# A hybrid SSD and attention layer on one core: grouped sample attention, a token-tile first norm, and a new link from w_out to the FFN

## The chip, the cores and the metric

The kernel runs on one core of a Trainium2 chip. The core has a matrix engine (PE, with its weight loads as PEld), a vector engine (DVE), a scalar engine (ACT), GpSimd (POOL), and DMA queues that are issued from SP, ACT or POOL. Each engine takes its instructions in the order of its own list and waits on semaphores for the others. The metric is the device time of one execution in microseconds (us).

## The reference

One step of a decoder layer on 256 prompt tokens and 8 sample tokens (one new token for each of 8 sequences), all in fp32:

```
hn     = rms_norm(x, norm_mix_pre)                    # (264, 2048)
q,k,v,z,xbc,dt,gates = split(hn @ w_in)
attn   = window attention with sinks, 32 heads of 64, 8 K/V heads, window 128
         (sample tokens: 127 cached keys and values of their own sequence, and the new one)
y      = SSD scan of the convolved xbc (prompt), one recurrent step (sample); gated group norm
merged = sigmoid(g_attn)*(attn @ w_attn_branch) + sigmoid(g_ssm)*(y @ w_ssm_branch)
h      = x + rms_norm(merged @ w_out, norm_mix_post)
f      = swiglu(rms_norm(h, norm_ffn_pre) @ w_gate_up) @ w_down
out    = h + rms_norm(f, norm_ffn_post)
```

The outputs are out for both kinds of tokens, and the new attention windows, convolution states and SSD states.

## The kernel before

Activations lie transposed: a matrix of 2048 channels by 264 tokens is 16 chunks of 128 channels by T = 264 tokens (tokens 0 to 255 prompt, 256 to 263 sample). Every product with a weight matrix goes through `gemm` (L142). A number a is split into hi, rounded for the matrix engine's fp32r format, and lo = a - hi, and a product takes three matmuls of a 128x128 weight block with 264 columns: hi·XH, hi·XL and lo·XH (L186 to L188). Per four blocks of rows one 1 MB DMA fills a `raw` buffer (SP's queue, three buffers); in two halves ACT makes `hi` (L176) and DVE makes `lo` (L177), then 24 matmuls a half follow. The whole kernel has 15984 of these matmuls. A matmul in plain fp32 runs in two passes and stands as two instructions in the trace (a transpose as one).

The order of the work is set by a scheduler that follows the program's text and estimated costs; `tc.manual_schedule` and `tc.issue_after` override it. Beside the gemms run generators on a list `side`; `gemm` calls `tick` (L129) after every four blocks, and that lets each generator take some steps.

Three places matter here.

**The start (L215 to L297).** Three tiles `xt` (sample, prompt 0 to 127, 128 to 255) are loaded on SP ahead of the first three raw blocks. ACT and DVE sum their squares (L263, L265). PE transposes each of the 16 chunks (three transposes a chunk, L272), ACT copies each to `xr` (L274), and SP stores it for later. `rsqrt` (L97) is three Newton steps on DVE; `rowcast` (L251) spreads the result over partitions by three fp32 matmuls of two passes each (L253), and DVE copies it to `rbx` (L280). Then DVE makes xf = xr·w·rbx (L283), ACT XH (L92), and POOL XL (L93). The first gemm makes the SSD's B, the second its C.

**Sample attention (L718 to L772), a generator beside the gemm of w_ssm_branch** (matmuls on YH, YL). For each of the 8 sequences: load K (ring `kr` of 3 on POOL's queue) and V, transpose K in four chunks (L732), four score matmuls with K as the stationary operand and 8 columns moving (L738), copy to `sT`. For every four sequences: transpose, softmax on 128 rows, one transpose back (L756), 16 matmuls of 8 columns with V as the stationary operand (L763), and 32 small copies into the attention output `AF` (L769).

**The link from w_out to the FFN (L845 to L919).** While w_out's chunks leave PSUM, ACT squares them and DVE adds the first 12 squares; after the last chunk 15 tiny matmuls (`tokstat`, L865) sum the squares over channels, `rsqrt` makes r1 on 3 columns, and `rowcast` spreads it. Then for each of 16 chunks, on DVE by hand-written order: mw·rb1 (L898), h = xr + mw (L900), HL (L908), with HH and a square on ACT (L901, L902) and a sum `hs` of squares on POOL (L904, L906). The first two column groups of w_gate_up, `gate(0)` and `gate(1)`, follow; their chunk order needs HH and HL one after the other, and their output is multiplied by rb2, the second norm, which two matmuls with a matrix of ones and an `rsqrt` on 264 columns make.

Of the kernel before, what the change touches and what calls it, by code (L numbers as in the profile page):

```python
# [32 lines left out]
def build(tc, I, O, wbufs=(3, 4, 4), gbufs=5, sbufs=((3,), (1,), (3,)), woff=0, aux="gpsimd", rr=1.4, pr=1.2, su=2, sr=1.0, hb=5, xbb=2, x0g=(0, 1, 2, 3), x0st="sync"):  # L33
# [91 lines left out]
    side = []  # L125
    last = [None]
# [19 lines left out]
    def gemm(W, segs, nk, X, perm_heads=False, perm_rows=False):  # L146
# [4 lines left out]
        for g0 in range(0, nk, 4):  # L151
            raw = til(wp, [P, 4, 512], "raw", wbufs[0])
            with tc.high_priority(offset=woff):
# [11 lines left out]
                for b in range(2):  # L165
# [13 lines left out]
            for b in range(2):  # L179
                hi, lo = hl[b]  # L180
                for m in range(nch):
                    for k in range(2):
# [3 lines left out]
                        PE.matmul(ps[m][:, :T], wh, XH[kc], start=f, stop=False)  # L186
# [28 lines left out]
    xts = {}  # L215
    N1 = til(A0, [P, P], "N1")
    for t in (2, 0, 1):
        n = NS if t == 2 else P
        xts[t] = til(A0, [P, D], f"xt{t}")
        dma(xts[t][:n], I["x_prompt"][t * P:t * P + P] if t < 2 else I["x_sample"])  # L220
        if t == 2:
            dma(ident, I["consts"][:, 0:P])
            dma(N1[0:16], I["norm_mix_pre"].rearrange("(c p) -> c p", p=P))
# [7 lines left out]
    ld(cst, I["consts"][:, P:])  # L231
# [15 lines left out]
    ps = sps()  # L247
    PE.transpose(ps[:, 0:16], N1[:16], ident[:16, :16])
    V.tensor_copy(w_pre, ps[:, 0:16])

    def rowcast(cols, ps):  # L251
        for t, n in enumerate((P, P, NS)):
            PE.matmul(ps[:, t * P:t * P + n], cols[:n, t:t + 1].broadcast_to([n, P]), ident[:n, :n], start=True, stop=True)  # L253
        return ps


    ss = til(cp, [P, 3], "ss")
    V.memset(ss, 1.0)
    for t in (2, 0, 1):
        n = NS if t == 2 else P  # L260
        sq = til(A0, [P, D], "sq", 2)
        if t == 1:
            V.tensor_tensor_reduce(sq, xts[t], xts[t], 1.0, 0.0, ALU.mult, ALU.add, ss[:, t:t + 1])  # L263
        else:
            S.activation(sq[:n], xts[t][:n], AF.Square, accum_out=ss[:n, t:t + 1])  # L265
    X0G = x0g
    X0ST = getattr(nc, x0st).dma_start
    xrs = []
    for c in range(16):
        ps = sps()  # L270
# [24 lines left out]
    PE.transpose(ps[:, 0:48], VR[:48], ident[:48, :48])  # L295
# [233 lines left out]
    AF_ = [til(AFp, [P, T], f"AF{c}") for c in range(16)]  # L529
# [188 lines left out]
    def sample_attention():  # L718
        for b4 in range(2):
            Vb = []  # L720
            sT = til(SA, [P, P], "sT", 1)
            for bb in range(4):
                b = 4 * b4 + bb
                kr = til(SA, [P, 512], "kr", 3)
                ld(kr, I["cache_win_k"][b])
                vb = til(SA, [P, 512], "vb", 4)
                ld(vb, I["cache_win_v"][b])
                ld(vb[0:1, :], vn_d[b:b + 1])
                Vb.append(vb)
# [27 lines left out]
            pt = til(SA, [P, P], "spt", 1)
            V.tensor_copy(pt, ps[:, 0:P])
# [42 lines left out]
    for g in range(8):  # L801
# [6 lines left out]
        for i in range(4):  # L808
            c = 4 * g + i
            V.scalar_tensor_tensor(y4[:, i, :], y4[:, i, :], w_ssmn[:, c:c + 1], rb, ALU.mult, ALU.mult)  # L810
            split(y4[:, i, :], YH[c], YL[c])
    side.append([sample_attention(), sr, 0.0])
    for u4 in range(4):
# [42 lines left out]
    mw = [til(EP, [P, T], f"mw{m}") for m in range(16)]  # L856
    xr = [til(EP, [P, T], f"xr{m}") for m in range(16)]
    for m in range(16):
        ld(xr[m], xT_d[m])
    halves = [lambda a: a[:, 0:2], lambda a: a[:NS, 2:3]]  # L860

    def tokstat(ps, accs, first, last):
        for t, n in enumerate((P, P, NS)):
# [251 lines left out]
```

## Time and profile before

| | |
|---|---|
| median of 3 runs | 2171.52 us (2171.44 to 2175.14) |
| the profiled execution | 2174.78 us |
| its span in the profile | 2173.0 us |
| PE busy | 2134.5 us, 98% of the span |
| DVE, ACT, POOL busy | 1380.0, 1105.6, 275.5 us |
| DMA | 442.52 MB, mean 204 GB/s |

Times in the profile count from the start of the span. In a timeline a row is a run of like instructions of one engine: start, time from the first's start to the last's end, engine, line, what it writes and reads, count, and in brackets the idle time before and who ended it. A matmul's duration is longer than its share of the engine, since matmuls overlap; its price is read from one start to the next. The column PEclk is the granted clock of the matrix engine, as a part of its full 2.4 GHz (0.50 is the lower level, 1.2 GHz).

### The profile page before, as it was taken

How to read it: one execution, taken by the hardware profiler on the slowest of the kernel's cores; microseconds unless marked ns; L12 is line 12 of the kernel's file. 1: busy time of each engine (PE TensorE's matmuls, PEld its weight loads, DVE VectorE, ACT ScalarE, POOL GpSimd, SP SyncE). 2: the span in 40 equal slices, each digit the busy share in tenths (PEclk: the TensorE clock that was granted, in tenths of full speed). 3: DMA queues.
4: the chain of work that ended last, by engine and by line, in shares of the span. 5: the costliest groups of instructions: out<-in, count | busy, mean ns of one | idle time of the engine just before them, and what ended most of it. 6: DMA issues, size and time to landing. Idle time of an engine off the chain costs nothing.

```text
span 2173.0 us, 43304 instructions
## 1 busy us (share of the span) xinstructions
PE 2134.5 (98%) x17533; PEld 2103.9 (97%) x17533; DVE 1380.0 (64%) x2764; ACT 1105.6 (51%) x1984; POOL 275.5 (13%) x512
## 2 busy tenths in 40 slices
PE   8999999999999999999999999899999999999997
PEld 6999999999999999999999999899999999999997
DVE  5877776777689988866544554844554545544444
ACT  5555555555478977755433444544444444434442
POOL 4100111111133222223001120300000000000000
PEclk9999999999999999999999999999999999999998
DMA  5655665555587787877567985365655555565552
GB/s 194 230 184 191 197 195 181 190 189 190 176 308 244 251 284 260 287 228 234 173 198 190 219 261 183 118 212 189 208 189 187 194 195 185 180 225 178 175 175 99
DMA packets 216633, 442.52 MB, mean 204 GB/s; under 512 B 12352, under 2 KB 28240, under 8 KB 215656
## 3 DMA queue, kind: packets, MB, share of 16 engines
q1 hardware_dynamic: 194864, 372.51, 53.2%
q0 software_dynamic: 21424, 67.17, 9.4%
q8 instruction: 137, 2.24, 0.4%
q14 instruction: 64, 0.52, 0.1%
q10 hardware_dynamic: 144, 0.07, 0.0%
HBM read 402.81 MB, written 41.45 MB: 204 GB/s over the span
## 4 chain that ended last, share of the span: by engine, by line
PE 91%; DMA 4%; DVE 3%; issue 1%; ACT 1%; POOL 0%; SPq 0%; DVEq 0%; ACTq 0%; POOLq 0%
PE g L186 28%; PE g L188 28%; PE g L187 28%; DMA raw<-in_w_attn_branch 2%; DMA y<-y_d 1%; PE s L272 1%; DVE lo L177 1%; PE w L701 1%; PE w L662 0%; PE w L694 0%; DMA ta_d<-tg 0%; DMA xt<-in_x_prompt 0%; ACT hi L176 0%; PE s L467 0%; DMA ts_d<-tg 0%
## 5 line engine op out<-in xcount | busy, mean ns | idle before, releaser
L177 DVE TENSOR_TENSOR lo<-raw,hi 128x1024 fp32r<-128x1024 f32 (+1 forms) x640 | 776.9, 1217 | 594.4 <-ACT hi L176 588.0
L176 ACT CAST hi<-raw 128x1024 fp32r<-128x1024 f32 (+1 forms) x640 | 663.6, 1040 | 850.7 <-PE g L187 767.7
L186 PE MATMUL g<-XH,hi 128*128 128x264 f32 x2192 | 630.8, 289 | 3.6 <-ACT tg L789 1.8
L187 PE MATMUL g<-XL,hi 128*128 128x264 f32 x2192 | 628.1, 287 | 0.0
L188 PE MATMUL g<-XH,lo 128*128 128x264 f32 x2192 | 626.1, 288 | 0.1
L186 PEld LDWEIGHTS g<-XH,hi 128*128 128x128 f32 x2192 | 413.9, 189 | 7.7 <-ACT tg L789 2.5
L187 PEld LDWEIGHTS g<-XL,hi 128*128 128x128 f32 x2192 | 414.2, 189 | 4.0 <-issue 3.5
L188 PEld LDWEIGHTS g<-XH,lo 128*128 128x128 f32 x2192 | 413.3, 189 | 3.5 <-issue 2.0
L187 PE MATMUL g<-HL,hi 128*128 128x264 f32 x1408 | 398.5, 285 | 2.1 <-DVE HL L908 2.1
L188 PE MATMUL g<-HH,lo 128*128 128x264 f32 x1408 | 397.6, 285 | 0.1
L186 PE MATMUL g<-HH,hi 128*128 128x264 f32 x1408 | 392.8, 286 | 1.8 <-ACT HH L901 1.8
L187 PEld LDWEIGHTS g<-HL,hi 128*128 128x128 f32 x1408 | 267.0, 190 | 3.0 <-DVE HL L908 3.0
L188 PEld LDWEIGHTS g<-HH,lo 128*128 128x128 f32 x1408 | 264.8, 189 | 0.4 <-DVE lo L177 0.3
L186 PEld LDWEIGHTS g<-HH,hi 128*128 128x128 f32 x1408 | 261.4, 188 | 1.8 <-ACT HH L901 1.8
L186 PE MATMUL g<-FH,hi 128*128 128x264 f32 x704 | 201.3, 286 | 0.0
L188 PE MATMUL g<-FH,lo 128*128 128x264 f32 x704 | 200.8, 286 | 0.0
L187 PE MATMUL g<-FL,hi 128*128 128x264 f32 x704 | 200.0, 284 | 0.0
L186 PE MATMUL g<-YH,hi 128*128 128x264 f32 x512 | 148.4, 292 | 0.9 <-ACT YH L92 0.9
L187 PE MATMUL g<-YL,hi 128*128 128x264 f32 x512 | 148.4, 290 | 0.7 <-DVE YL L93 0.7
L188 PE MATMUL g<-YH,lo 128*128 128x264 f32 x512 | 148.4, 290 | 0.0
L186 PEld LDWEIGHTS g<-FH,hi 128*128 128x128 f32 x704 | 132.9, 189 | 0.0
L188 PEld LDWEIGHTS g<-FH,lo 128*128 128x128 f32 x704 | 132.5, 188 | 0.0
(415 smaller groups left out, 3021.4 us busy)
## 6 DMA issues: line engine op xcount, KB each, us to landing
raw<-in_w_in SPq DMA_DIRECT2D x136, 1024.0 KB, 5.3
raw<-in_w_gate_up SPq DMA_DIRECT2D x88, 1024.0 KB, 5.0
raw<-in_w_down SPq DMA_DIRECT2D x44, 1024.0 KB, 5.1
raw<-in_w_ssm_branch SPq DMA_DIRECT2D x32, 1024.0 KB, 5.2
h<-in_state_ssm POOLq DMA_DIRECT2D x64, 256.0 KB, 5.3
out_ssm_sample<-h POOLq DMA_DIRECT2D x64, 256.0 KB, 4.9
raw<-in_w_attn_branch SPq DMA_DIRECT2D x32, 512.0 KB, 10.7
raw<-in_w_out SPq DMA_DIRECT2D x16, 1024.0 KB, 5.1
```

The lines of the kernel that those rows point to most:

```text
L176: S.copy(hi[:, :, :w], r)
L177: V.tensor_tensor(lo[:, :, :w], r, fr(hi[:, :, :w]), ALU.subtract)
L186: PE.matmul(ps[m][:, :T], wh, XH[kc], start=f, stop=False)
L187: PE.matmul(ps[m][:, :T], wh, XL[kc], start=False, stop=False)
L188: PE.matmul(ps[m][:, :T], wl, XH[kc], start=False, stop=l)
L272: PE.transpose(ps[:, t * P:t * P + n], xts[t][:n, c * P:(c + 1) * P], ident[:n, :n])
L701: PE.matmul(pw[jj[j], q, 384:512], Vk[:, k, vc[j]], pT[j][:, (q + k) * P:(q + k + 1) * P], start=f, stop=l)
```

## The change

**Start.** x_prompt's tiles are loaded in halves on SP, first of all; x_sample, `ident` and N1 go to ACT's queue, and the constants `cst` are loaded later, on SP. The order of PE, ACT and DVE is written by hand. Seven fp32 matmuls on zeros (`busy`) stand ahead of the transposes, 3 ahead of the broadcast and 2 behind it. Four transposes share a PSUM tile, which one copy of 128x512 empties (DVE for prompt tile 0, ACT for tile 1). The sums' rsqrt goes to all partitions by three transposes of a column that is broadcast, and stays in PSUM. DVE makes all of XL. The first gemm's splits get an explicit place between the norm's operations.

**Sample attention.** The roles are exchanged: Q (32 columns, zero-padded) is stationary and K moves with 128 columns, so that the four chunks c write the partitions 32c to 32c+31 of one PSUM tile; likewise the four sequences in the product with V, with 512 columns moving. Softmax is done for four sequences at once, and there are three yields a group more. The K ring has 2 buffers, the V loads come first, in a new pool.

**Link.** The squares are summed up to chunk 13, so that 3 tiny matmuls come after the last chunk (9 in all); r1 is on 10 columns; two transposes broadcast it. Dummy fp32 matmuls (`spin`, 264 columns, 4 and 2) stand before and behind. From the third chunk on DVE's products and sums take two chunks an operation. Squares on ACT, the sum on POOL and the 264-column rsqrt of the second norm are gone: `tokens`, a generator beside `gate(1)`, squares h in token-major tiles as it copies them, and makes r2 on 10 columns and rb2 by two transposes. The outputs of `gate(0)` and `gate(1)` are only copied; after both, 8 products with rb2 and 8 Silus follow.

```diff
-    for t in (2, 0, 1):
-        ...
-        dma(xts[t][:n], I["x_prompt"][t * P:t * P + P] if t < 2 else I["x_sample"])
+    for t in range(2):
+        for c0 in range(0, D, XC):          # XC = 1024
+            dma(xts[t][:, c0:c0 + XC], I["x_prompt"][t * P:t * P + P, c0:c0 + XC])
+    S.dma_start(xts[2][:NS], I["x_sample"])
...
-    for c in range(16):
-        ps = sps()
-        for t, n in enumerate((P, P, NS)):
-            PE.transpose(ps[:, t * P:t * P + n], xts[t][:n, c * P:(c + 1) * P], ident[:n, :n])
-        xr = til(A0, [P, T], "xr", 16)
-        S.copy(xr, ps[:, :T])
-        X0ST(xT_d[c], xr)
+        def busy(n):
+            for _ in range(n):
+                PE.matmul(pw[:, 0:NP], wz[:, 0:P], wz, start=True, stop=True)
+        def turn(t, k):
+            ps = gps()
+            for c in range(4 * k, 4 * k + 4):
+                PE.transpose(ps[:, (c % 4) * P:(c % 4 + 1) * P], xts[t][:, c * P:(c + 1) * P], ident)
+            return XR[:, 4 * k:4 * k + 4, t * P:(t + 1) * P], ps[:, :].rearrange("p (c n) -> p c n", c=4)
+        busy(7)
+        ...
+        busy(3)
+        rs = rsqrt(cp, [(lambda a: a, ss)], P, 3, 1.0 / D, EPS, "rx")
+        rbx = gps()
         for t, n in enumerate((P, P, NS)):
+            PE.transpose(rbx[:, t * P:t * P + n], rs[:n, t:t + 1].broadcast_to([n, P]), ident[:n, :n])
+        busy(2)
...
-        split(xf, XH[c], XL[c], E=G if c % 4 in X0G else V)
+        a, b = split(xf, XH[c], XL[c])
...
+                kr = til(SB, [P, 512], "kw", 2)
...
-                    PE.matmul(pS[:, c * 8:c * 8 + 8], kt[:, c, :], QB[:, b, c, :], start=True, stop=True)
+                    PE.matmul(pS[32 * c:32 * c + 32, bb * P:(bb + 1) * P], QP[:, bb, c, :], kt[:, c, :], start=True, stop=True)
...
-                for c in range(4):
-                    sl = slice(bb * 32 + c * 8, bb * 32 + c * 8 + 8)
-                    PE.matmul(po[:, sl], Vb[bb][:, c * P:(c + 1) * P], pt[:, sl], start=True, stop=True)
+                PE.matmul(po[32 * bb:32 * bb + 32, :], pt[:, bb].rearrange("p c r -> p (c r)"), Vb[bb], start=True, stop=True)
...
+            if 0 < m < 14:
+                V.tensor_tensor(sa, sa, q, ALU.add)
+            elif m >= 14:
+                ins = sumsq(pst, [sa, q] if m == 14 else [q], 16 * (m - 14))
-    tokstat(ps, [sa] + qs, True, True)
-    r1 = rsqrt(cp, [(f, f(ps)) for f in halves], P, 3, 1.0 / D, 4 * EPS, "r1")
-    rb1 = rowcast(r1, sps())[:, :T]
+    ins = spin(ins, 4)
+    r1 = rsqrt(cp, [(lambda a: a, total(pst, "r1s"))], P, 2 + NS, 1.0 / D, 4 * EPS, "r1")
+    ...
+            ins = PE.transpose(rb1[:, t * P:(t + 1) * P], r1[:, t:t + 1].broadcast_to([P, P]), ident)
+    spin(ins, 2)
...
+        for c0, n in ((0, 1), (1, 1), (2, 2), (4, 2), (6, 2), (8, 2), (10, 2), (12, 2), (14, 2), (16, 0)):
+            if n:
+                m, x = MW[:, c0:c0 + n], XO[:, c0:c0 + n]
+                V.tensor_tensor(m, m, rb1[:, :T].unsqueeze(1).broadcast_to([P, n, T]), ALU.mult)
+                V.tensor_tensor(x, x, m, ALU.add)
+                ...
+            for c in prev:
+                V.scalar_tensor_tensor(HL[c], XO[:, c], w_fpre[:, c:c + 1], fr(HH[c]), ALU.mult, ALU.subtract)
```

DVE's list just behind the first norm's rsqrt, before (`lo` and `hi` are halves of the first gemm's weight blocks, `xf` the normalized chunks, `xr` the transposed x):

```order
L115 SCALAR_TENSOR_TENSOR rxy_286<-rxt_287,rxy_286 128x3
L280 COPY rbx_283<-g_300 128x264
L177 TENSOR_TENSOR lo_396<-raw_393,hi_395 128x1024
L177 TENSOR_TENSOR lo_400<-raw_393,hi_399 128x1024
L283 SCALAR_TENSOR_TENSOR xf_305<-xr_175,w_pre_155,rbx_283 128x264
L283 SCALAR_TENSOR_TENSOR xf_309<-xr_182,w_pre_155,rbx_283 128x264
L283 SCALAR_TENSOR_TENSOR xf_313<-xr_189,w_pre_155,rbx_283 128x264
L177 TENSOR_TENSOR lo_454<-raw_451,hi_453 128x1024
L177 TENSOR_TENSOR lo_458<-raw_451,hi_457 128x1024
L283 SCALAR_TENSOR_TENSOR xf_317<-xr_196,w_pre_155,rbx_283 128x264
```

The same place now (`XR` holds all transposed x, `g_272` is rbx in PSUM):

```order
L115 SCALAR_TENSOR_TENSOR rxy_258<-rxt_259,rxy_258 128x3
L310 SCALAR_TENSOR_TENSOR xf_283<-XR_165,w_pre_158,g_272 128x264
L310 SCALAR_TENSOR_TENSOR xf_287<-XR_165,w_pre_158,g_272 128x264
L310 SCALAR_TENSOR_TENSOR xf_291<-XR_165,w_pre_158,g_272 128x264
L93 TENSOR_TENSOR XL_5_87<-xf_283,XH_4_86 128x264
L93 TENSOR_TENSOR XL_7_89<-xf_287,XH_6_88 128x264
L180 TENSOR_TENSOR lo_354<-raw_351,hi_353 128x1024
L310 SCALAR_TENSOR_TENSOR xf_295<-XR_165,w_pre_158,g_272 128x264
L310 SCALAR_TENSOR_TENSOR xf_299<-XR_165,w_pre_158,g_272 128x264
L93 TENSOR_TENSOR XL_9_91<-xf_291,XH_8_90 128x264
```

The copy of rbx is gone, the first weight half comes behind three xf and two XL instead of ahead of the first xf, and the XL stand on DVE, two and two.

PE's list in the middle of the sample attention, where the first four sequences end, before (`spt` are the transposed probabilities, `vb` is V, `kr` is K, `g` rows are the gemm of w_ssm_branch):

```order
L188 MATMUL g_12886<-YH_1908_12727,lo_13407 128x264
L186 MATMUL g_12887<-YH_1906_12725,hi_13406 128x264
L187 MATMUL g_12887<-YL_1907_12726,hi_13406 128x264
L188 MATMUL g_12887<-YH_1906_12725,lo_13407 128x264
L763 MATMUL s_13273<-spt_13271,vb_12949 128x8 x4
L763 MATMUL s_13273<-spt_13271,vb_13026 128x8 x4
L763 MATMUL s_13273<-spt_13271,vb_13103 128x8 x4
L763 MATMUL s_13273<-spt_13271,vb_13180 128x8 x4
L732 MATMUL s_13386<-ident_67,kr_13381 128x128 x4
```

The same place now:

```order
L196 MATMUL g_12853<-YH_1879_12700,lo_13383 128x264
L192 MATMUL g_12854<-YH_1877_12698,hi_13382 128x264
L195 MATMUL g_12854<-YL_1878_12699,hi_13382 128x264
L798 MATMUL s_13298<-vb_12917,spt_13296 32x512
L798 MATMUL s_13298<-vb_12920,spt_13296 32x512
L798 MATMUL s_13298<-vb_12923,spt_13296 32x512
L798 MATMUL s_13298<-vb_12926,spt_13296 32x512
L196 MATMUL g_12854<-YH_1877_12698,lo_13383 128x264
L192 MATMUL g_12854<-YH_1879_12700,hi_13382 128x264
```

Sixteen matmuls of 8 columns, with the next K's transposes right behind them, are now four of 512 columns with gemm work behind; the next K's transposes come 25 gemm matmuls later.

DVE's list where the link's rsqrt ends and the chunks begin, before:

```order
L115 SCALAR_TENSOR_TENSOR r1y_17420<-r1t_17421,r1y_17420 128x3
L898 TENSOR_TENSOR mw_2409_16351<-mw_2409_16351,s_17436 128x264
L898 TENSOR_TENSOR mw_2410_16352<-mw_2410_16352,s_17436 128x264
L900 TENSOR_TENSOR xr_2425_16367<-xr_2425_16367,mw_2409_16351 128x264
L898 TENSOR_TENSOR mw_2411_16353<-mw_2411_16353,s_17436 128x264
L900 TENSOR_TENSOR xr_2426_16368<-xr_2426_16368,mw_2410_16352 128x264
L908 SCALAR_TENSOR_TENSOR HL_2377_16313<-xr_2425_16367,vecs_156,HH_2376_16312 128x264
L898 TENSOR_TENSOR mw_2412_16354<-mw_2412_16354,s_17436 128x264
L900 TENSOR_TENSOR xr_2427_16369<-xr_2427_16369,mw_2411_16353 128x264
L908 SCALAR_TENSOR_TENSOR HL_2379_16315<-xr_2426_16368,vecs_156,HH_2378_16314 128x264
```

The same place now (`xo` is h):

```order
L115 SCALAR_TENSOR_TENSOR r1y_17290<-r1t_17291,r1y_17290 128x10
L951 TENSOR_TENSOR mw_16258<-mw_16258,s_17304 128x264
L952 TENSOR_TENSOR xo_16259<-xo_16259,mw_16258 128x264
L951 TENSOR_TENSOR mw_16258<-mw_16258,s_17304 128x264
L952 TENSOR_TENSOR xo_16259<-xo_16259,mw_16258 128x264
L956 SCALAR_TENSOR_TENSOR HL_2335_16220<-xo_16259,vecs_159,HH_2334_16219 128x264
L951 TENSOR_TENSOR mw_16258<-mw_16258,s_17304 128x528
L952 TENSOR_TENSOR xo_16259<-xo_16259,mw_16258 128x528
L956 SCALAR_TENSOR_TENSOR HL_2337_16222<-xo_16259,vecs_159,HH_2336_16221 128x264
L951 TENSOR_TENSOR mw_16258<-mw_16258,s_17304 128x528
L952 TENSOR_TENSOR xo_16259<-xo_16259,mw_16258 128x528
```

Four operations instead of five stand ahead of the first HL, and from the third chunk on a product or sum takes two chunks.

## Rows read from the trace of the kernel before

**Rows 1.** The page: busy us by engine, share of the span, instructions.
```profile
PE 2134.5 (98%) x17533; PEld 2103.9 (97%) x17533; DVE 1380.0 (64%) x2764; ACT 1105.6 (51%) x1984; POOL 275.5 (13%) x512
```
**Rows 2.** Windows: us, PE, PEld, DVE, ACT, POOL busy (instructions), PEclk, DMA.
```profile
31.50:51.80 20.30, 20.30 (x165) 20.09 (x165) 14.86 (x19) 9.23 (x19) 11.80 (x15) 1.00 0.16 43
61.10:66.00 4.90, 4.82 (x25) 4.61 (x26) 4.80 (x6) 3.60 (x6) 0.00 (x0) 0.65 0.95 320
...
1011.10:1018.00 6.90, 6.90 (x35) 6.90 (x35) 2.36 (x9) 2.83 (x10) 3.59 (x7) 0.51 0.68 189
1052.00:1055.40 3.40, 3.40 (x18) 3.40 (x18) 2.76 (x12) 3.09 (x12) 0.00 (x0) 0.53 0.00 0
...
1371.50:1376.50 5.00, 4.97 (x22) 4.98 (x23) 5.00 (x11) 3.30 (x9) 3.36 (x7) 0.50 0.00 0
1376.50:1403.10 26.60, 24.39 (x188) 23.20 (x187) 25.63 (x43) 16.60 (x32) 17.91 (x24) 1.00 0.37 120
```
**Rows 3.** Timelines of the start, PE, DVE and POOL.
```profile
11.52 6.81 PE L272 MATMUL s<-ident,xt 128*128 128x128 f32 x24 [3.09 <-DMA xt<-in_x_prompt]
18.25 1.74 PE L253 MATMUL g<-ident,rxy 128*128 128x128 f32 x6
...
20.03 0.43 DVE L280 COPY rbx<-g 128x264 f32<-128x264 f32 x1 [3.86 <-PE g L253]
...
24.91 4.22 POOL L93 TENSOR_TENSOR XL<-xf,XH 128x264 fp32r<-128x264 f32 x4 [18.27 <-ACT XH L92]
...
61.16 0.39 PE L186 MATMUL g<-XH,hi 128*128 128x264 f32 x1 [1.75 <-ACT hi L176]
```
**Rows 4.** Timelines of PE beside the attention and the recurrence.
```profile
138.34 1.02 PE L433 MATMUL s<-X,Bk 128*128 128x512 f32 x2
...
139.32 0.29 PE L188 MATMUL g<-XH,lo 128*128 128x264 f32 x1
...
689.63 0.88 PE L701 MATMUL w<-pt,Vk 128*64 128x128 f32 x12
690.43 0.39 PE L188 MATMUL g<-XH,lo 128*128 128x264 f32 x1
...
1005.31 0.30 PE L756 MATMUL s<-ident,pe 128*128 128x128 f32 x1 [1.23 <-DVE pe L754]
...
1008.26 4.08 PE L763 MATMUL s<-spt,vb 128*128 128x8 f32 x32
...
1018.86 0.95 PE L738 MATMUL s<-QB,kt 128*128 128x8 f32 x8
1019.67 0.64 PE L732 MATMUL s<-ident,kr 128*128 128x128 f32 x4
```
**Rows 5.** Line L725, K's loads on POOL's queue.
```profile
DMA to landing us min/median/max: 3.0/3.6/7.5
```
**Rows 6.** Timelines of DVE and PE at the link.
```profile
1365.79 0.21 DVE L106 TENSOR_SCALAR r1x<-s 128x2 f32<-128x2 f32 x2 [0.55 <-PE s L865]
...
1369.81 0.77 DVE L898 TENSOR_TENSOR mw<-mw,s 128x264 f32<-128x264 f32 x2 [1.84 <-PE s L253]
1370.50 0.43 DVE L900 TENSOR_TENSOR xr<-xr,mw 128x264 f32<-128x264 f32 x1
...
1362.47 0.28 PE L865 MATMUL s<-cst,sa 128*128 128x1 f32 x2
...
1371.53 0.81 PE L186 MATMUL g<-HH,hi 128*128 128x264 f32 x2 [1.75 <-ACT HH L901]
```
**Rows 7.** DVE by form, 1365 to 1404 us: busy us, mean ns, idle before.
```profile
L900 DVE TENSOR_TENSOR xr<-xr,mw 128x264 f32<-128x264 f32 x16 | 10.4, 648 | 0.0
L908 DVE SCALAR_TENSOR_TENSOR HL<-xr,vecs,HH 128x264 fp32r<-128x264 f32 x16 | 10.3, 645 | 0.2 <-ACT HH L901 0.2
L177 DVE TENSOR_TENSOR lo<-raw,hi 128x1024 fp32r<-128x1024 f32 x7 | 8.5, 1215 | 0.8 <-ACT hi L176 0.8
L898 DVE TENSOR_TENSOR mw<-mw,s 128x264 f32<-128x264 f32 x16 | 6.6, 419 | 1.8 <-PE s L253 1.8
```

More of the change, by code (lines that the diff above doesn't have):

```diff
@@ L174, in gemm @@
                             V.tensor_tensor(lk, rk, fr(hk), ALU.subtract)
+                    elif behind is not None:
+                        with tc.issue_after(behind[0][g0 + 2 * b]):
+                            S.copy(hi[:, :, :w], r)
+                        with tc.issue_after(behind[1][g0 + 2 * b]):
+                            V.tensor_tensor(lo[:, :, :w], r, fr(hi[:, :, :w]), ALU.subtract)
                     else:
@@ L281, in build @@
+    for c in range(0, 16, 4):
+        st(xT_d[c:c + 4].rearrange("c p t -> p c t"), XR[:, c:c + 4, :])
+    first = {0: xr_end.ins}, {}
     for c in range(16):
@@ L395, in build @@
             for nm, c0 in (("B", C_B), ("C", C_C)):
-                with tc.issue_after(rb_end.ins):
-                    pss = gemm(win, [(c0 + g * P, 512)], 16, X)
+                pss = pss0 if g == 0 and nm == "B" else gemm(win, [(c0 + g * P, 512)], 16, X)
                 for i in range(4):
@@ new lines, in sample_attention @@
+            S.copy(pc, po[:, :])
+            yield
+            ps = sps(1)
+            for c in range(4):
+                PE.transpose(ps[:, c * P:(c + 1) * P], pc[:, c * P:(c + 1) * P], ident)
+            for c in range(4):
+                pv = ps[:, c * P:(c + 1) * P].rearrange("p (b c j i) -> p c j i b", b=4, c=4, j=2)[:, c]
+                for j in range(2):
+                    jj = slice(64 * j, 64 * j + 64)
+                    (S.copy if j else V.tensor_copy)(AFb[jj, 4 * c:4 * c + 4, NP + 4 * b4:NP + 4 * b4 + 4], pv[jj, j])
@@ L855, in build, with sumsq, total, spin @@
     EP = pool("ep")
[L856 to L863, printed above, removed]
-            for k, a in enumerate(accs):
-                PE.matmul(ps[:n, t:t + 1], a[:, t * P:t * P + n], ones[:, 0:1], start=first and k == 0, stop=last and k == len(accs) - 1)
-    def stats(acc, pl):
-        qs = []
-        def add(m, src):
-            q = acc if m == 0 else til(pl, [P, T], "sqe", 4)
-            S.activation(q, src, AF.Square)
-            if 0 < m < 12:
-                V.tensor_tensor(acc, acc, q, ALU.add)
-            elif m >= 12:
-                qs.append(q)
-        return qs, add
+    MW = til(EP, [P, 16, T], "mw")
+    XO = til(EP, [P, 16, T], "xo")
+    for m in range(0, 16, 4):
+        ld(XO[:, m:m + 4], xT_d[m:m + 4].rearrange("c p t -> p c t"))
+    def sumsq(pst, accs, o):
+        for t in range(2):
+            for k, a in enumerate(accs):
+                PE.matmul(pst[:, o + t:o + t + 1], a[:, t * P:(t + 1) * P], ones[:, 0:1], start=k == 0, stop=k == len(accs) - 1)
+        for k, a in enumerate(accs):
+            ins = PE.matmul(pst[:, o + 2:o + 2 + NS], ones, a[:, NP:T], start=k == 0, stop=k == len(accs) - 1)
+        return ins
+    def total(pst, tag):
+        a, b = (til(cp, [P, 2 + NS], tag + x) for x in "ab")
+        V.tensor_copy(a, pst[:, 0:2 + NS])
+        V.tensor_tensor(b, pst[:, 16:18 + NS], a, ALU.add)
+        return b
+    def spin(after, n):
+        for _ in range(n):
+            with tc.issue_after(after.ins):
+                after = PE.matmul(pz[:, 0:T], ident, cosT, start=True, stop=True)
+        return after
     sa = til(EP, [P, T], "sa")
-    qs, add = stats(sa, EP)
+    pst = sps()
     for u4 in range(4):
@@ L987, in build @@
     pst = sps()
-    def sumsq(accs, o):
-        for t in range(2):
-            for k, a in enumerate(accs):
-                PE.matmul(pst[:, o + t:o + t + 1], a[:, t * P:(t + 1) * P], ones[:, 0:1], start=k == 0, stop=k == len(accs) - 1)
-        for k, a in enumerate(accs):
-            PE.matmul(pst[:, o + 2:o + 2 + NS], ones, a[:, NP:T], start=k == 0, stop=k == len(accs) - 1)
     for u4 in range(4):
```

244 lines of the change are left out of this document (132 added, 112 removed).

## The prediction

> **What bounds the kernel now.** I read the page first: PE is busy 98% of the span, no other engine over 64% [rows 1]. So only PE's time counts: its stretches without gemm work, its stretches at the lower clock, and its small matmuls. The reader is to see in the windows [rows 2] what a gemm matmul costs when nothing disturbs it: 165 in 20.30 us, 0.123 each. All 15984 at that price are 1966 us, so some 207 us of 2173.0 are something else, and the change reaches three pieces of it. Of the timelines I then read the ends of these pieces: who ended PE's idle time.
>
> All sums are made against the profiled execution, 2174.78 us with a span of 2173.0; the median of the runs is 3.26 us lower, and I take that off at the end.
>
> **Start.** The transposes run one every 6.81 / 24 = 0.28 us, the broadcast's six passes take 1.74 us, and rbx is there at 20.03 + 0.43 = 20.5 [rows 3]. From there the B gemm needs until 51.8, the end of its window [rows 2]: 31.3 us. POOL makes an XL in 4.22 / 4 = 1.06 us [rows 3], while a subtraction of that size on DVE goes at 0.69 / 2 = 0.345 [rows 6]. The order shows that all of it now hangs on DVE: 16 xf at 0.43 (as the copy of that size, L280), 16 XL at 0.345 and 8 halves at 1.215 [rows 3, 6, 7], 6.9 + 5.5 + 9.7 = 22.1 us, and about 4 us behind it for the last 24 matmuls at 0.123 and the first operations: 26.1 from rbx. That saves 5.2 us even with an unmoved rbx.
>
> When is rbx there? The transposes of tile 1 wait for its load until 11.52 [rows 3], which is issued earlier now. If PE stays at its low pace, 32 large transposes at 0.28 and the small ones, dummies and broadcast bring rbx to 20.3: no gain there. If the dummies bring the high pace (four transposes in 0.64 us beside the recurrence, [rows 4], so 0.12 to 0.16 each), the load, the rsqrt and the rest end at 13.9. Between ends so far apart I take 17.5, a gain of 3.0. Then C: PE is idle 1.75 us before it, and 25 matmuls take 4.9 us in a stretch with a clock of 0.65 [rows 2, 3], where 0.123 would make 3.1. The constants no longer stand in its way; I take 2.3 of these 3.6. Start: 5.2 + 3.0 + 2.3 = 10.5, bounds 5.4 (rbx at 20.3, and C as before) and 5.2 + 6.6 + 3.6 = 15.4.
>
> The clock column reads 1.00 in the prologue, though transposes take more than twice their later price, so it settles nothing there. The Trainium skill ("TensorE: Matmul & The Clock Gate", Part 4, PE-mode transpose) says that transposes do not count as busy for the clock gate. By that rule the dummies' effect would be gone before rbx, and the start would give its lower bound. The rows agree so far as 24 transposes at 0.28 did not speed up among themselves.
>
> **Sample attention.** Before: 32 instructions of L763 in 4.08 us, twice, and eight of L738 in 1019.67 − 1018.86 = 0.81 us, eight times [rows 4]: 8.2 + 6.5 = 14.7 us. After: the scores are 64 instructions with 128 columns, the products with V 16 with 512 columns, and there are 14 more transposes (1.7 us). No row shows four column groups. Serial prices: 0.101 for 128 columns (as the 8-column ones), and (139.32 − 138.34 − 0.12) / 2 = 0.43 for 512 [rows 4]: 6.5 + 6.9 + 1.7 = 15.1, a loss of 0.4. Nearest row: matmuls into groups of 64 columns go at (690.43 − 689.63) / 12 = 0.067, two thirds of the serial price [rows 4]: 4.3 + 4.6 + 1.7 = 10.6, a gain of 4.1. All four side by side: 1.6 + 1.7 + 1.7 = 5.0, a gain of 9.7. I take the nearest row, 4.1.
>
> The same page, Part 3 (Packing small matmuls), gives 2.38 times for three column groups with 512 columns. By an estimate with that factor the sum would be 7.3 us in place of 10.6, and the forecast 3.3 lower; no row here shows it.
>
> Behind the bursts of 8 columns the clock falls: 6.9 us at 0.51 and 3.4 us at 0.53 [rows 2], a loss of 3.4 + 1.6 = 5.0 us. Wide matmuls take the bursts' place, so I take these as gone; if the clock falls all the same, nothing. PE stands 1.23 us for the probabilities at L756 [rows 4], twice; the yields put gemm work there, 2.5. Against it: the K ring is shorter, K's second load of the last half stands on POOL's queue behind stores that wait for DVE (a landing takes 3.6 us, [rows 5]; up to 1.6 of it on PE), and at the gemm's head PE now waits for the copy of K before YL (1.2): −2.8. Sum 4.1 + 5.0 + 2.5 − 2.8 = 8.8; bounds −0.7 (serial, clock falls) and 17.2 (side by side, no cost).
>
> **Link.** w_out's last matmul starts next to 1362.47, gate(0) ends at 1403.1: 40.6 us [rows 2, 6], for 192 matmuls that need 23.6. DVE's first step waits for tokstat until 1365.79, the first product waits 1.84 us for the broadcast, and the first matmul comes at 1371.53 [rows 6]. With 3 tiny matmuls behind the last square the rsqrt starts when DVE is through with w_out's last chunk, 0.5 earlier; two transposes in place of six passes save about 1.2; one operation less ahead of the first HL is hidden behind HH. So the first matmul comes at 1369.7. Then DVE: 16 times three operations cost 10.4 + 10.3 + 6.6 = 27.3 us, of which the first two ran at 0.65 instead of 0.345 and 0.41, beside POOL's sums [rows 6, 7]. POOL's sums are gone: 16 × (0.345 + 0.345 + 0.41) = 17.6, and 6 halves at 1.215 = 7.3, together 24.9 from 1368.4, or 1393.3. That two chunks share an operation I cost at no gain. PE's own work from 1369.7 ends at 1393.3 as well. That is 9.8 earlier, if the clock stays up. In the profile 22 matmuls took 5.0 us at 0.50 [rows 2]; if it falls again, 2.3 to 2.8 are lost, and 7.0 remain. Later there is a cost: gate(1) carries the token tiles (8 copies and 8 squares on ACT) and r2, and 8 products and Silus stand in one burst behind it, 0 to 2 us. I take 7.5; bounds 4.8 and 9.8.
>
> **Sum.** 10.5 + 8.8 + 7.5 = 26.8: 2174.78 − 26.8 = 2148.0, and less 3.26 it is 2144.7, rounded to 2145.
>
> **Rivals.**
> 1. *The clock falls wherever it fell.* Dummies and transposes don't hold it, neither at the start (5.4) nor behind the sample attention (8.8 − 5.0 = 3.8) nor at the link (7.0 − 2.0 = 5.0). For it: in every one of these places it fell [rows 2], and the skill's rule above. Against it: the link's dummies are ordinary fp32 matmuls that stand exactly in the gap. 14.2 us of gain, 2157.
> 2. *Everything bites.* Four groups run side by side, the clock holds, only K's cost of 2.8 stays: 15.4 + 14.4 + 9.0 = 38.8, so 2133. For it: 64-column groups do overlap already [rows 4].
> 3. *The regrouping does nothing.* The groups run one after another, 4.5 less than forecast: 22.3, so 2149. It is inside the forecast's own range.
> 4. *Slower: the K ring.* With two buffers a K load can only start when the transposes two sequences earlier are done, and it stands in POOL's queue. Six of the eight loads can be late; PE runs in order, and each late one stops it for up to a landing of 7.5 us [rows 5] (45 us, and 2171.5 − 26.8 + 45 = 2190). It decides from 26.8 / 6 = 4.5 us a load on. Against it: between a load's release and its use the order leaves some 90 gemm matmuls at 0.123, 11 us.
>
> **How the numbers follow.** Forecast with rival 3: 60%, own range 2139 to 2151. Rival 1: 20%. Rival 2: 13%. Rival 4: 4%, and 3% for no change. A difference under 0.2% (4.3 us) can't be told from none. Faster: 60 + 20 + 13 less 3 for mishaps in them = 0.90; same 0.04; slower 0.06. The range reaches to both of the first two rivals: all lower bounds together (5.4 − 0.7 + 4.8 = 9.5) give 2162, rival 2 gives 2133.
>
> **What would show it.** Right: rbx's reader (the first xf) starts near 17.5, the C gemm near 52 instead of 61; transposes of the start cost under 0.2 us; no stretch near 0.5 in PEclk between 1000 and 1050 and behind w_out; four products with V in under 3.5 us; gate(0) over 31 us after w_out. Wrong: transposes at 0.28 up to rbx; a stretch at 0.5 behind the dummies; PE waiting for K's DMA at the transposes of K; PE idle in gate(1) for ACT; idle time between 600 and 960 us, where the scheduler laid the attention anew and PE hardly waits now.

## The result and the profile after

The changed kernel takes 2145.62 us (median of 4 runs, 2143.39 to 2147.37) against 2172.23 us before (4 runs, 2171.44 to 2175.14): a ratio of 0.9875, 95% interval [0.9857, 0.9892]. The forecast was 2145, the range 2133 to 2162. The profiled executions are 2174.78 us before and 2147.37 us after, 27.4 us apart, with spans of 2173.0 and 2145.6.

Where the 27.4 us lie is read from the first and last matmul of each product. These are rows of a view by tile: instructions with count, the shortest, median and longest duration in ns, and the start of the first and the last. First the kernel before (XH is w_in, YH w_ssm_branch, MH w_out, HH w_gate_up):

```profile
L188 PE MATMUL g<-XH,lo x2192: 278/284/587, 28.2 to 956.9; 128*128 128x264 f32 x200
...
L186 PE MATMUL g<-YH,hi x512: 279/285/568, 958.5 to 1171.8; 128*128 128x264 f32 x171
L188 PE MATMUL g<-YH,lo x512: 280/284/422, 960.0 to 1172.1; 128*128 128x264 f32 x171
...
L188 PE MATMUL g<-MH,lo x256: 281/284/289, 1269.0 to 1362.3; 128*128 128x264 f32 x128
...
L186 PE MATMUL g<-HH,hi x1408: 278/283/587, 1371.5 to 1896.2; 128*128 128x264 f32 x176
L188 PE MATMUL g<-HH,lo x1408: 280/284/422, 1372.8 to 1896.4; 128*128 128x264 f32 x176
```

The same rows after:

```profile
L196 PE MATMUL g<-XH,lo x2192: 278/284/396, 18.6 to 945.5; 128*128 128x264 f32 x200
...
L192 PE MATMUL g<-YH,hi x512: 278/283/422, 947.1 to 1150.0; 128*128 128x264 f32 x171
L196 PE MATMUL g<-YH,lo x512: 278/284/422, 950.3 to 1150.3; 128*128 128x264 f32 x171
...
L196 PE MATMUL g<-MH,lo x256: 280/284/292, 1248.3 to 1341.4; 128*128 128x264 f32 x128
...
L192 PE MATMUL g<-HH,hi x1408: 278/283/387, 1350.4 to 1869.6; 128*128 128x264 f32 x176
L196 PE MATMUL g<-HH,lo x1408: 280/284/368, 1351.3 to 1869.9; 128*128 128x264 f32 x176
```

Up to the end of w_in 11.4 us are won (956.9 to 945.5). The w_ssm_branch stretch falls from 213.6 to 203.2, 10.4 more. w_attn_branch and w_out give 0.9 back (190.2 to 191.1). From w_out's last matmul to the first of the FFN it is 9.2 and 9.0: nearly nothing, where 1.8 were forecast. w_gate_up falls from 524.9 to 519.5, 5.4, and what follows by 0.9. That is 27.4. One execution each stands behind these figures: in another one of the changed kernel (e10 below) w_in ends at 941.4 and w_attn_branch takes 101.9 us where it takes 97.5 here, so a part of a few us in these two stretches can be chance.

**Start.** Timelines of PE and DVE after:

```profile
1.11 5.11 PE L270 MATMUL s<-wz 128*128 128x256 f32 x14 [1.11 <-POOL wz L224]
7.24 1.94 PE L275 MATMUL g<-ident,xt 128*128 128x128 f32 x16 [1.02 <-DMA ident<-in_consts]
9.20 1.15 PE L287 MATMUL s<-ident,xt 8*128 8x8 f32 x16
10.27 1.97 PE L275 MATMUL g<-ident,xt 128*128 128x128 f32 x16
...
16.38 0.75 PE L192 MATMUL g<-XH,hi 128*128 128x264 f32 x4
...
50.02 0.39 PE L192 MATMUL g<-XH,hi 128*128 128x264 f32 x1 [1.08 <-ACT hi L182]
...
15.39 1.29 DVE L310 SCALAR_TENSOR_TENSOR xf<-XR,w_pre,g 128x264 f32<-128x264 f32 x3 [0.82 <-PE g L302]
```

The transposes take 0.12 us each instead of 0.28 [rows 3], xf starts at 15.39, and C's first matmul comes at 50.02 instead of 61.16: 11.1 us.

**Sample attention.** Timeline of PE after; a price is the distance to the next row's start:

```profile
971.41 0.43 PE L775 MATMUL s<-kt,QP 128*32 128x128 f32 x8
971.76 0.39 PE L192 MATMUL g<-YH,hi 128*128 128x264 f32 x1
...
1001.38 1.07 PE L798 MATMUL s<-vb,spt 128*32 128x512 f32 x8
1002.38 0.39 PE L196 MATMUL g<-YH,lo 128*128 128x264 f32 x1
```

Eight score instructions take 0.35 us, 0.044 each; eight products with V 1.00, 0.125 each. Both are far under the nearest row of before, 0.067 and two thirds of 0.43 [rows 4]. And of three falls of the clock in the stretch one is left, at its head. Windows after, columns as in [rows 2]:

```profile
950.50:955.50 5.00, 5.00 (x31) 5.00 (x31) 1.73 (x6) 1.19 (x5) 2.68 (x4) 0.68 0.89 259
...
1010.00:1050.00 40.00, 40.00 (x344) 37.80 (x345) 17.87 (x26) 18.48 (x35) 3.22 (x6) 1.00 0.57 191
```

**Link.** Timelines of PE and DVE, windows, and DVE by form, after:

```profile
1343.06 0.35 PE L905 MATMUL s<-cst,sa 128*128 128x1 f32 x2 [1.35 <-DVE sa L934]
...
1344.84 0.37 PE L907 MATMUL s<-sqe,cst 128*128 128x8 f32 x2
...
1350.42 0.75 PE L192 MATMUL g<-HH,hi 128*128 128x264 f32 x4
...
1341.68 0.89 DVE L932 TENSOR_SCALAR mw<-g,vecs 128x264 f32<-128x264 f32 x2
1342.48 0.43 DVE L934 TENSOR_TENSOR sa<-sa,sqe 128x264 f32<-128x264 f32 x1
...
1345.24 0.17 DVE L912 COPY r1sa<-s 128x10 f32<-128x10 f32 x1 [0.79 <-PE s L907]
...
1348.92 0.43 DVE L951 TENSOR_TENSOR mw<-mw,s 128x264 f32<-128x264 f32 x1 [1.05 <-PE s L944]
```

```profile
1341.50:1350.30 8.80, 7.08 (x36) 5.35 (x34) 6.52 (x24) 1.95 (x4) 0.00 (x0) 0.81 0.49 165
1350.30:1352.50 2.20, 2.20 (x19) 2.17 (x19) 2.17 (x5) 0.66 (x3) 0.00 (x0) 1.00 0.00 0
```

```profile
L956 DVE SCALAR_TENSOR_TENSOR HL<-xo,vecs,HH 128x264 fp32r<-128x264 f32 x16 | 7.2, 490 | 0.0
L951 DVE TENSOR_TENSOR mw<-mw,s 128x528 f32<-128x528 f32 x7 | 4.9, 701 | 0.0
```

The clock falls inside the gap (0.81 over it) but is at 1.00 from the first FFN matmul on, the broadcast costs 1.05 instead of 1.84, and without POOL's sums HL takes 490 ns instead of 645 [rows 6, 7]. But PE's tiny matmuls wait 1.35 us for the sum of squares, which stands on DVE behind two mw, and the rsqrt's first operation starts 3.8 us behind the start of w_out's last matmul instead of 3.5 (1341.4 to 1345.24, 1362.3 to 1365.79). And all nine tiny matmuls stand behind w_out's last one, not three as planned: from 1343.06 on they take another 2.0 us of PE.

### The profile page after: what moved, and what is told of

It reads as the page before. It is cut to its first block, busy times and chain, and to the rows that moved or that the text cites. A ratio compares the mean times of both kernels' runs of the same rounds, so it can differ in the third digit from the quotient of the medians.

```text
span 2145.6 us, 43115 instructions
## 1 busy us (share of the span) xinstructions
PE 2116.6 (99%) x17512; PEld 2083.6 (97%) x17512; DVE 1369.1 (64%) x2748; ACT 1105.0 (52%) x1969; POOL 234.2 (11%) x462
## 4 chain that ended last, share of the span: by engine, by line
PE 91%; DMA 5%; DVE 2%; issue 1%; ACT 1%; SPq 0%; POOL 0%; DVEq 0%; ACTq 0%; POOLq 0%
PE g L192 28%; PE g L196 28%; PE g L195 28%; DMA raw<-in_w_attn_branch 1%; DMA out_ssm_sample<-h 1%; DMA h<-in_state_ssm 1%; DMA ta_d<-tg 0%; PE w L735 0%; ACT hi L182 0%; PE w L728 0%; DMA xt<-in_x_prompt 0%; PE w L696 0%; PE s L499 0%; DMA raw<-in_w_in 0%; DVE lo L183 0%
## 5 line engine op out<-in xcount | busy, mean ns | idle before, releaser
L183 DVE TENSOR_TENSOR lo<-raw,hi 128x1024 fp32r<-128x1024 f32 (+1 forms) x632 | 765.4, 1214 | 595.5 <-ACT hi L182 594.2
L192 PE MATMUL g<-XH,hi 128*128 128x264 f32 x2192 | 624.4, 288 | 2.3 <-ACT hi L182 1.1
L196 PE MATMUL g<-XH,lo 128*128 128x264 f32 x2192 | 619.7, 287 | 1.7 <-DVE lo L183 1.0
L196 PEld LDWEIGHTS g<-XH,lo 128*128 128x128 f32 x2192 | 408.9, 188 | 5.3 <-issue 1.9
L195 PEld LDWEIGHTS g<-FL,hi 128*128 128x128 f32 x704 | 132.8, 189 | 0.0
## 6 DMA issues: line engine op xcount, KB each, us to landing
raw<-in_w_attn_branch SPq DMA_DIRECT2D x32, 512.0 KB, 10.6
```

The lines of the kernel that those rows point to most:

```text
L183: V.tensor_tensor(lo[:, :, :w], r, fr(hi[:, :, :w]), ALU.subtract)
L192: ins = PE.matmul(ps[m][:, :T], wh, XH[kc], start=f, stop=False)
L195: PE.matmul(ps[m][:, :T], wh, XL[kc], start=False, stop=False)
L196: PE.matmul(ps[m][:, :T], wl, XH[kc], start=False, stop=l)
```

## Experiments

**The three parts alone.** e1, e2 and e3 are the kernel before with one part each.

> The kernel before with the changed start alone. If the three parts add up as the two traces stand (the X gemms end 11.4 us earlier after the change), it is 11 us faster: 2160.5 to 2161.5, first xf near 15.4, C's first matmul near 50. Rival: part of the 11.4 us comes from the scheduler laying the attention phase anew, then 9 to 10 us, and the window from 600 us to the end of the X gemms keeps its old length.

> The kernel before with the changed sample attention alone. If the parts add: the stretch of the w_ssm_branch gemm goes from 213.6 to about 203.2 us, 10 us faster, near 2162. Rival (the gain there hangs on the changed state in which the new start leaves the scheduler): less than 6 us. Score matmuls at 0.045 an instruction, four products with V in 1.0 us.

> The kernel before with the changed link alone (one small tile lies in another pool). If the parts add: 5.5 to 6.5 us faster, near 2166; first FFN matmul 9 us after w_out's last one as before, and no stretch of the gemm at the lower clock behind it. Rival: the link's gain is in the earlier first matmul, as forecast: then first matmul 7.2 us behind w_out and 7.5 to 9.8 us faster.

Ratios: start 0.9933 [0.9917, 0.9950], 2159.37 us; attention 0.9941 [0.9926, 0.9956], 2161.36; link 0.9975 [0.9963, 0.9987], 2167.81; before beside them 2173.87. That is 14.5, 12.5 and 6.1 us, 33.1 together where the whole won 26.6; with intervals of 2.6 to 3.6 us on each the parts may still add up. A hint that they don't quite: the stretch of w_attn_branch takes 94.9 to 97.4 us in the six kept traces of the kernel before and of e1 to e3, e8 and e9, but 95.8 to 102.4 in the eight of the changed kernel and its variants, some 3 us more on average. No run shows why. In the traces the w_ssm_branch stretch of e2 is 202.2 us (956.3 to 1158.5), and e3's first FFN matmul comes 8.6 us behind w_out's last, both as the theory had it. In e1's trace w_in ends 11.1 us earlier (945.8), so its rival is out. What its time has beyond that lies in the w_ssm_branch stretch, 210.4 us with the old attention, where the clock fell behind one of the two bursts of products with V (the L763 of before), not behind both. So e1's surplus is no part of the start.

**e4: no dummies at the start.**

```diff
-        busy(7)
...
-        busy(3)
...
-        busy(2)
```

> The changed kernel without the twelve dummy matmuls of the start. Theory: the seven ahead of the transposes raise the clock and the transposes keep it: without them the 32 large transposes take 0.28 us each instead of 0.12, the first xf comes 4 to 5 us later and the kernel takes 4 to 6 us more, near 2150.5. Rival: the transposes raise the clock by themselves, or the dummies are not what did it: transposes at 0.12, time within 1 us of 2145.6, or 1 us less for the two dummies ahead of the first gemm matmul.

2146.76 us, ratio 0.9873 [0.9859, 0.9888]: no difference to the changed kernel. The theory was half right. PE's timeline and a window of e4:

```profile
7.23 3.65 PE L275 MATMUL g<-ident,xt 128*128 128x128 f32 x16 [7.23 <-DMA ident<-in_consts]
...
11.96 1.97 PE L275 MATMUL g<-ident,xt 128*128 128x128 f32 x16
...
17.01 0.77 PE L192 MATMUL g<-XH,hi 128*128 128x264 f32 x4 [1.12 <-ACT XH L92]
...
52.84 0.39 PE L192 MATMUL g<-XH,hi 128*128 128x264 f32 x1 [0.67 <-ACT hi L182]
```

```profile
17.00:24.00 7.00, 6.76 (x30) 6.30 (x31) 6.94 (x16) 5.08 (x10) 0.00 (x0) 0.54 1.04 393
```

The first 16 transposes run at 0.23, the last 16 at 0.12 with nothing but transposes ahead of them: they raise the pace by themselves. The first matmul comes only 0.6 us later; then the clock is at 0.54 for 7 us, and C begins at 52.84, 2.8 us later than with the dummies. That is their price in the trace. At the end of w_in 1.2 us of it are left (946.7 against 945.5), less than two executions of the changed kernel differ there (945.5 and 941.4), and the medians don't show it.

**e8 and e9: what made the old start long.** e8 is the kernel before with XL on DVE; e9 is the kernel before with the 8-row transposes of the sample tile taken together.

```diff
-        split(xf, XH[c], XL[c], E=G if c % 4 in X0G else V)
+        split(xf, XH[c], XL[c])
```

```diff
...
+    for c in range(16):
+        PE.transpose(ps[:, 8 * c:8 * c + 8], xts[2][:NS, c * P:(c + 1) * P], ident[:NS, :NS])
+    S.copy(XR[:, :, NP:T], ps[:, 0:128].rearrange("p (c n) -> p c n", c=16))
     for c in range(16):
         ps = sps()
-        for t, n in enumerate((P, P, NS)):
+        for t, n in enumerate((P, P)):
...
```

> The kernel before with one edit: XL of the start on DVE instead of POOL. Theory: POOL's 1.06 us an XL and its collisions with DVE set the length of the first gemm from rbx on (31.3 us): it becomes 26 to 27 us and the kernel 4 to 5 us faster, near 2168. Rival: the gain of the start lies in the earlier rbx and the loads alone, DVE being as full as POOL was slow: less than 1.5 us.

> The kernel before with one edit at the start: the 16 transposes of the 8 sample tokens stand together ahead of the others in one PSUM tile (one more ACT copy), and a chunk has two transposes of 128 rows. Theory: PE's 14 us of transposes, ahead of the first gemm matmul at 26.4, set the length of the start, since the first gemm then runs nearly at PE's full pace; a chunk takes 0.82 us now and would take 0.45 to 0.5 without the switch between 128-row and 8-row transposes, so the first gemm matmul comes 3.5 to 5 us earlier and so does all behind it: 2167.5 to 2169. Rival: the lower clock alone makes the 0.82 us (a chunk then falls to no less than 0.75) or ACT's copies or the square sums bind: less than 1.5 us.

e8: 2171.87 us, ratio 0.9995 [0.9985, 1.0004]; the rival's number holds. The forecast's reason for the first 5.2 us, POOL's XL, falls. Windows of e8 show why:

```profile
26.00:31.00 5.00, 5.00 (x27) 4.53 (x27) 4.70 (x15) 1.87 (x5) 0.00 (x0) 1.00 0.96 295
31.00:36.00 5.00, 5.00 (x41) 4.93 (x41) 5.00 (x14) 3.63 (x7) 0.00 (x0) 1.00 0.13 40
36.00:41.00 5.00, 5.00 (x43) 5.00 (x42) 5.00 (x11) 3.65 (x6) 0.00 (x0) 1.00 0.20 54
41.00:46.00 5.00, 5.00 (x43) 5.00 (x42) 1.89 (x3) 0.60 (x3) 0.00 (x0) 1.00 0.21 56
```

PE is full from its first gemm matmul on, and DVE, against the rival's reason, is done early. The same is in [rows 2] (165 matmuls in 20.30 us): B's 192 matmuls take PE's own pace, so B's first output is there some 25 us behind its first matmul. PE and ACT before, and ACT after:

```profile
19.93 5.81 PE L272 MATMUL s<-ident,xt 128*128 128x128 f32 x21
...
26.36 1.25 PE L186 MATMUL g<-XH,hi 128*128 128x264 f32 x4
...
50.96 0.37 ACT L311 COPY R<-g 128x256 f32<-128x256 f32 x1 [0.45 <-PE g L188]
...
41.18 0.37 ACT L344 COPY R<-g 128x256 f32<-128x256 f32 x1 [1.37 <-PE g L196]
```

Before the change 21 transposes stand on PE behind the broadcast, and the first gemm matmul waits for them. It moved from 26.4 to 16.4, 10.0 us, and ACT's first copy of B's output by 9.8.

e9: 2170.87 us, ratio 1.0001 [0.9991, 1.0011]: no change by its times. PE's timeline of e9:

```profile
11.04 4.19 PE L277 MATMUL s<-ident,xt 128*128 128x128 f32 x17 [2.77 <-DMA xt<-in_x_prompt]
...
19.25 1.54 PE L277 MATMUL s<-ident,xt 128*128 128x128 f32 x6 [2.49 <-ACT XR L278]
...
24.24 1.25 PE L186 MATMUL g<-XH,hi 128*128 128x264 f32 x4
```

A transpose falls to 0.25, but now PE waits for ACT's copies, which stand behind weight halves, and the first matmul comes 2.1 us earlier, not 3.5 to 5. By this trace grouping the small transposes is a part of the start's gain, the smaller one; how the rest divides between earlier loads, four transposes a tile and copies on two engines wasn't tried.

**e6: one column group.**

```diff
...
-                    PE.matmul(pS[32 * c:32 * c + 32, bb * P:(bb + 1) * P], QP[:, bb, c, :], kt[:, c, :], start=True, stop=True)
+                    PE.matmul(pS[0:32, bb * P:(bb + 1) * P], QP[:, bb, c, :], kt[:, c, :], start=True, stop=True)
...
-                PE.matmul(po[32 * bb:32 * bb + 32, :], pt[:, bb].rearrange("p c r -> p (c r)"), Vb[bb], start=True, stop=True)
+                PE.matmul(po[0:32, :], pt[:, bb].rearrange("p c r -> p (c r)"), Vb[bb], start=True, stop=True)
```

Two memsets a half, of pS and po, are left out here.

> The changed kernel with all score matmuls and all products with V in one column group (partitions 0 to 31; three quarters of the results are overwritten, and two memsets a half stand on DVE). Theory: the price of 0.045 and 0.125 us an instruction comes from four groups side by side, so in one group they go at 0.10 and 0.43: 64 x 0.056 + 16 x 0.305 = 8.5 us more, near 2154. Rival: a matmul with 32 stationary columns is that cheap by itself: within 1.5 us of 2145.6 and the same prices.

2157.02 us, ratio 0.9927 [0.9913, 0.9942]: 11.4 us over the changed kernel, for 8.5 expected. PE's timeline of e6:

```profile
976.69 1.06 PE L776 MATMUL s<-kt,QP 128*32 128x128 f32 x8
977.68 0.39 PE L192 MATMUL g<-YH,hi 128*128 128x264 f32 x1
...
1000.82 3.62 PE L800 MATMUL s<-vb,spt 128*32 128x512 f32 x8
1004.37 0.39 PE L196 MATMUL g<-YH,lo 128*128 128x264 f32 x1
```

0.124 and 0.444 us an instruction: 64 × 0.080 + 16 × 0.319 = 10.2 us, near what the stretch shows (946.5 to 1160.3, 213.8 instead of 203.2). So the four groups do run side by side, 2.8 times as fast as one for the scores and 3.6 times for V. In e6 the results also overwrite each other; that this adds to the price isn't ruled out, but the 0.444 is what 512 columns took before without it (0.43, [rows 4]).

**e5, e7, e10 to e12: the link.** e5 leaves out the six dummies; e7 moves the last four mw to ACT, behind the last square.

```diff
-    ins = spin(ins, 4)
...
-    spin(ins, 2)
```

```diff
+    late = []
...
-            S.activation(q, ps[:, :T], AF.Square)
+            sqi = S.activation(q, ps[:, :T], AF.Square)
...
-                V.tensor_scalar(MW[:, m], ps[:, :T], w_post[:, m:m + 1], None, ALU.mult)
+                late.append((m, ps))
...
+    for m, ps in late:
+        with tc.issue_after(sqi.ins):
+            S.mul(MW[:, m], ps[:, :T], w_post[:, m:m + 1])
```

> The changed kernel without the six dummy matmuls of the link. Theory: these hold the clock through the gap, so without them the first 20 or so FFN matmuls run at 0.22 us as before the change and it takes 2.3 to 2.8 us more, near 2148.2. Rival: the tiny matmuls, the transposes and the shorter rsqrt chain leave the clock up by themselves: no difference, 2145.6, or up to 0.5 less since the dummies delay the broadcast's transposes.

> The changed kernel with the last four products mw = w_out's chunk times its weight on ACT, behind the last square, instead of DVE. Theory: the link's rsqrt starts late because DVE does these products ahead of the last sums of squares (PE waits 1.35 us for sa): it starts 3.74 us behind w_out's last matmul now, and 2.3 to 2.6 with the edit, so 1.2 us less, near 2144.4. Rival: the tiny matmuls at 0.22 us each or ACT set it: no change.

e5: 2143.29 us, ratio 0.9872 [0.9857, 0.9888]; its times show no difference. Its window shows the mechanism:

```profile
1350.30:1355.30 5.00, 5.00 (x23) 4.76 (x24) 4.90 (x11) 2.62 (x6) 0.00 (x0) 0.50 0.00 0
```

Without the dummies the clock is at 0.50 behind the gap, as before the change. But w_gate_up takes 520.8 us (1350.7 to 1871.5), 1.3 more than with them and not 2.3 to 2.8. DVE is busy 4.90 of 5.00 us, so a faster PE would perhaps wait for it in part; no run tests that.

e7: 2140.84 us, ratio 0.9853 [0.9836, 0.9869]. PE's timeline of e7:

```profile
1340.98 0.35 PE L905 MATMUL s<-cst,sa 128*128 128x1 f32 x2 [0.34 <-DVE sa L935]
...
1348.09 0.75 PE L192 MATMUL g<-HH,hi 128*128 128x264 f32 x4
```

The wait for sa falls from 1.35 to 0.34 us, and the first FFN matmul comes 8.0 us behind the start of w_out's last hi matmul (1340.1) instead of 9.2 (1341.2 to 1350.4). So DVE's order held the rsqrt back, by 1.0 of its 3.8 us (2.8 in e7, 1340.37 to 1343.17); most of the rest are the nine tiny matmuls. e11 repeats e7 beside the changed kernel (e10); to e7's edit e12 adds longer rings for the loads of w_attn_branch's chunks.

```diff
-            t = til(DP, [P, T], "ts", 3)
-            m1 = til(DP, [P, T], "m1", 3)
+            t = til(DP, [P, T], "ts", 6)
+            m1 = til(DP, [P, T], "m1", 6)
```

> The changed kernel again, beside the two below on one chip: 26 to 28 us faster than the kernel before.

> The changed kernel with the last four products mw on ACT, again. If the 2 us that the first matmul of the FFN gained on w_out's last one hold in the median, it is 2 us faster than the changed kernel beside it; the rival is that this was the spread between executions (under 0.7 us).

> As the one before, and the rings of the loads for w_attn_branch's chunks (ta and m1) have 6 buffers in place of 3. Theory: PE's idle time in that gemm (2.1 us, and a stretch of 22 matmuls at the lower clock behind it) comes from these loads, which start late: 2 to 3 us less. Rival: they stand behind a store on POOL's queue, and the DMA engines are busy all the time there, so more buffers change nothing or crowd out the weights: 0 to 1 us more.

Changed kernel 2145.29 us, 0.9881 [0.9866, 0.9896]; e11 2142.73, 0.9870 [0.9856, 0.9885]; e12 2141.65, 0.9870 [0.9855, 0.9885]. The medians are 2.6 and 3.6 us lower, but the intervals overlap, as that of e7 does with the changed kernel's. What the traces show is the 1.2 us: from the start of w_out's last hi matmul to the first FFN matmul it is 8.0 us in e7, e11 and e12, and 9.2 in both executions of the changed kernel. That the whole kernel is faster by it isn't shown by the times, though its median is lower each time. The rings can't be told from nothing.

## Why the forecast was right, step by step

**The sum.** 26.8 us were forecast and 27.4 measured between the profiled executions. So close a sum is partly luck: the start came out 0.6 above its forecast and the sample attention 1.6, the link 1.9 below, and inside each part some terms were wrong.

**Start (10.5 forecast, 11.1 at C's first matmul).** The size was right, the main step was not. rbx is there 5.1 us earlier (15.4) where 3.0 were taken, from rbx to B's first output it takes 4.7 less where 5.2 were forecast, and C gives 1.4 where 2.3 were. But the 5.2 "even with an unmoved rbx" rested on DVE and POOL setting B's length; e8 shows that PE sets it. The 4.7 are PE's: its first gemm matmul came 5.9 us behind rbx, behind 21 transposes, and now comes 1.0 us behind it. The Trainium skill (TensorE: Matmul & The Clock Gate, Part 4, PE-mode transpose) says that transposes don't count as busy in the same way for the clock gate; by that the start would give 5.4. e4 doesn't agree: its last 16 transposes ran at 0.12, twice the pace of the first, with only transposes ahead. In the kernel before, 24 in a row with every third of 8 rows had stayed at 0.28 [rows 3]; what makes the difference is open.

**Sample attention (8.8 forecast, 10.4).** The term of 4.1 was mis-sized. The scores take 64 × 0.044 = 2.8 us and the products with V 16 × 0.125 = 2.0. The added transposes are 12, not 14 (36 before, 48 after), or 1.5 us. That is 6.3 in place of 10.6, a gain of 8.4. Taking two groups of 64 columns as the nearest row was too careful. By an estimate with the Trainium skill's factor of 2.38 for three groups (TensorE: Matmul & The Clock Gate, Part 3, Packing small matmuls) the sum had been 7.3, nearer; the factors measured here, for four groups, are 2.8 and 3.6. The 5.0 of the clock came: both falls behind the bursts are gone. The 2.5 for waits at L756 was half of that, since the second never waited. The cost of 2.8 was there in another form: PE waits 1.57 us ahead of the first scores, at the head. These terms add to 13.0. Of the 2.6 too much 0.7 is my price of L763: its bursts took 3.94 and 3.49 us to the next row, not 4.08 each. The rest I can't place.

**Link (7.5 forecast, 5.6).** The step that the rsqrt starts "0.5 earlier" failed: it starts 0.3 later, behind DVE's mw and nine tiny matmuls where three were counted on, and with an added operation and wider columns r1 comes later still. That eats the 0.8 saved at the broadcast (1.2 forecast), and the first product starts 7.5 us behind w_out's last matmul as before. e7 shows DVE's order as a cause. So of the 1.8 forecast for the first matmul 0.2 came. Behind it the forecast had 8.0 more (9.8 less 1.8), with up to 2.8 of them at risk with the clock, and w_gate_up gave 5.4. The 8.0 was too large: up to 1403.1 PE does 204 gemm matmuls and 4 with the matrix of ones, not gate(0)'s 192 alone. What could be won there is, as an estimate from [rows 2], the 2.2 us in which PE is idle and the 2.3 to 2.8 of the clock. Of the 5.4 the dummies' share is 1.3 (e5); the 4.1 that are left fit DVE without POOL beside it, since PE no longer waits for HL (2.1 us before), but no run tests that alone. Two chunks an operation gain nothing: 0.70 us for 528 columns, where two of 264 take 0.69 [rows 6]. No cost showed in gate(1).

**Rivals.** In the places of rival 1 the clock fell only inside the link's gap, and was up again at its end, so that rival is out. Rival 2 had the groups right, rival 3 wrong (e6). Rival 4 did not come: in the changed kernel's waits PE stands nowhere for a load of K.

## What to carry to other kernels

Before a stretch is put down to a slow engine, look whether the engine that sets the end is full in it: B's window was full on PE, so work moved off POOL did not shorten it, and its earlier start was the gain. Matmuls with 32 stationary columns gain by lying in different column groups. A chain of small steps starts with the last operand of its first one: what stands ahead of that operand on its own engine is moved away first.

## What the runs showed of the hardware

Four column groups of 32 run 2.8 times (128 columns) and 3.6 times (512 columns) as fast as one group, in two-pass fp32 matmuls (e6). Transposes alone brought PE from 0.23 to 0.12 us each within 16 of them and 16 small ones (e4). Behind the same bursts of 8-column matmuls the clock fell twice in one execution (0.51 and 0.53) and once in another (e1), so such a fall is no fixed price. In the link's gap of 9 us the six dummies did not keep the clock up all the time (0.81 over the gap), but had it at 1.00 at the first FFN matmul; without them it was at 0.50 for the next 5 us (e5). And executions of one kernel differ by some us: the stretch of w_attn_branch took 97.5 us in one of the changed kernel and 101.9 in another (e10), where PE waited 2.1 and 4.9 us for DVE.
